# Hybrid decoder layer on one core: bias table written in the down-projection, other PSUM pairs for the third plain product, half-row token loads and a reordered first block of both feed-forward stages

## The chip, the cores and the metric

The program runs on one core of one Trainium2 chip, in one launch. The metric is the device time of the whole program in microseconds (us), the median of repeated executions. One further execution was recorded by the hardware profiler; all rows shown here are from that one.

## The reference, cut to what matters

One layer for 1024 prompt tokens and 8 sample tokens (1032 columns in all, width 1024, everything in float32): a feed-forward half step, a mixer (windowed attention and retention behind gates), a second feed-forward half step. A layer norm follows each of the three.

```
hp = layer_norm(ALPHA * hp + 0.5 * swiglu(hp, ffn1_w_up, ffn1_w_down), ln1_g, ln1_b)
mp = prompt_mixers(hp, w_in, sinks, rel_bias, w_attn_out, w_ret_out, w_o)     # likewise for the samples
hp = layer_norm(ALPHA * hp + mp, ln2_g, ln2_b)
hp = layer_norm(ALPHA * hp + 0.5 * swiglu(hp, ffn2_w_up, ffn2_w_down), ln3_g, ln3_b)

def swiglu(x, w_up, w_down):                 # w_up: 1024 x 5632, w_down: 2816 x 1024
    gate, up = split(x @ w_up, 2)
    return (silu(gate) * up) @ w_down
bias = rel_bias[rel_bucket(dist)]            # 8 heads, read by the windowed attention
```

## The kernel before, in words

**Operands.** Each float32 operand is split into a high part (`hi`, rounded to the matmul's format by ACT) and a low part (`lo = x - hi`, by DVE). A product is three matmuls: `w_hi*hi`, `w_hi*lo`, `w_lo*hi`. Weights arrive in halves of 128x512 (256 KB) in four buffers `raw`, are split into eight slots `w_hi`/`w_lo`, and are issued by SP's queue. A `raw` buffer is loaded again when the DVE split of its last use is through.

**The up-projections.** The 2816 hidden columns are 22 tiles (`ft` 0 to 21) of 128 gate and 128 up columns. The tokens are halved (`HT` = 516 columns) and so is the width: `ya` holds rows 0 to 511 of x, `yb` rows 512 to 1023, which gives four blocks b11, b12 (from `ya`) and b21, b22 (from `yb`). Tiles 1 to 21 use a seven-product scheme for 2x2 blocks: product units `P(ft, i)`, i = 0 to 6, each 24 matmuls of 128x258 with one of seven prepared token tiles `TT[i]` and one weight quarter or a sum of quarters (`st`, made by `sums` on DVE from the four `raw` buffers). Tile 0 is computed plainly as four units `C0` to `C3` of 48 matmuls, which need only tokens that are split and not summed; behind them DVE makes the sums that the other `TT` need. `t_stage(i)` emits the subtraction (in place in `ya`) and the two splits of one token tile.

The order of units, written by hand, is C0, C1, P(1,0), P(1,1), C2, C3, then P(1,3), P(1,2), P(1,4), P(1,5), P(1,6), P(2,0) and so on in order. C0 and C1 read TT[0] and TT[1], C2 and C3 TT[6] and TT[5].

**Accumulators.** Three PSUM pairs `pr[0..2]` take the products. C units alternate between pairs 0 and 2; P units of an odd tile use pair 1 for i = 0, 2, 4, 6, pair 0 for i = 1 and pair 2 for i = 3, 5 (an even tile swaps 0 and 1). A pair can be overwritten only when ACT or DVE has read it (the "evacuation").

**Order on the engines.** The program is emitted by hand in one pass. `Emit` keeps a modelled time `E.pe`, which decides only where a side task's instructions are placed; on the chip every engine takes its instructions in the order emitted. `before(ui, u)` emits what a unit needs ahead of it: token stages, weight splits (`need(o)`), and the functions held back until buffers are free (`held_th`: the gates; `held_ut`: stores).

**Side tasks.** `bias_tables` multiplies the head biases with a one-hot matrix and has POOL's queue write the result, widened, to a scratch tensor `scr` in DRAM: eight transfers of 128 rows of 1 KB. The attention reads it much later (`fill_att`). It starts when `E.pe` is over 60. `alpha_b` scales `yb` on POOL for the residual. `ln_last` is the layer norm of the last 264 columns ahead of the second feed-forward; `env["aside"]` is work that it lets in while it waits.

**The down-projections** take 4 hidden tiles a group in units of 12 matmuls into four PSUM banks `mb`, DVE adds each into `ya`/`yb`; weights come as before, 2 halves per 72 matmuls, and the activations are read back from DRAM (`T<-adr`).

```
order += [(1, i) for i in (3, 2, 4, 5, 6)]
order += [(ft, i) for ft in range(2, NF) for i in range(7)]
...
bank = pr[(al, 1 - al, al, 2, al, 2, al)[u["i"]] if u["kind"] == "P" else u["i"] % 2 * 2]
```

## Time and profile before

| | |
|---|---|
| median of 3 runs | 2252.5 us (2250.31 to 2253.45) |
| the profiled execution's own time | 2248.05 us |
| its span, first to last instruction | 2246.0 us |
| mean granted TensorE clock | 0.985 of full |
| PE busy | 2165.3 us (96% of the span) |
| DVE, ACT, POOL busy | 1369.7, 772.4, 236.0 us |
| PE's longest wait in the first 80 us, and the wait ahead of P(1,3) in the second feed-forward | 8.56 us, 4.51 us |

PE, the matmul engine, is the one that is nearly always at work, so what a change is worth is read from the places where PE stands still or runs at the lower clock. The count of matmuls in a stretch, held against the count in an undisturbed stretch, shows both at once. A row of the trace gives start, duration, engine, line, output and inputs, and in brackets how long the engine had been idle and what ended that.

### The profile page before, as it was taken

Reading aid. Unit: us, or ns where it says so; the run is one execution under the profiler, and the core shown is the slowest. Engines: PE = TensorE matmul, PEld = TensorE weight load, DVE = VectorE, ACT = ScalarE, POOL = GpSimd, SP = SyncE. Lnnn points to the kernel's source line nnn. Section 1 sums busy time; section 2 is a strip of 40 time slices with the busy share of each in tenths; the row PEclk is TensorE's granted clock in tenths of the full one; section 3 lists DMA queues with packets and bytes.
Section 4 is the critical chain, followed back from the end, with each engine's and each line's share of the span. In section 5 each row is a group of like instructions: output and inputs, shape, how many; then the busy total and the mean of one; then the engine's idle time right before and its main releaser. Section 6 shows DMA issues by size and latency. Waiting matters only on the chain.

```text
span 2246.0 us, 38320 instructions
## 1 busy us (share of the span) xinstructions
PE 2165.3 (96%) x15381; PEld 2133.5 (95%) x15381; DVE 1369.7 (61%) x2561; ACT 772.4 (34%) x1477; POOL 236.0 (11%) x290
## 2 busy tenths in 40 slices
PE   7979999999999899999999999997999999999996
PEld 6979999999999889999979999997999999999996
DVE  6746666654334887566665856778666666553337
ACT  4424333431111576111233443645434343411113
POOL 1200000001002434111110201111000000010003
PEclk8989999999999999999999999998999999999998
DMA  3553223357330210111164343541333233494212
GB/s 130 108 100 109 105 95 109 109 213 297 111 116 29 65 41 29 49 40 40 40 184 146 122 145 127 181 131 48 123 109 109 104 102 102 148 364 142 83 43 76
DMA packets 104851, 253.84 MB, mean 113 GB/s; under 512 B 13162, under 2 KB 16962, under 8 KB 98258
## 3 DMA queue, kind: packets, MB, share of 16 engines
q1 hardware_dynamic: 103970, 250.31, 32.5%
q0 software_dynamic: 704, 1.09, 1.5%
q8 instruction: 121, 1.98, 0.4%
q14 instruction: 56, 0.46, 0.1%
HBM read 194.95 MB, written 57.45 MB: 112 GB/s over the span
## 4 chain that ended last, share of the span: by engine, by line
PE 83%; DVE 8%; DMA 3%; ACT 3%; issue 2%; POOL 1%; SPq 0%; ACTq 0%; DVEq 0%; POOLq 0%
PE mb L90 43%; PE pr L90 37%; DMA raw<-in_w_dram 3%; PE sb L90 2%; DVE T L112 1%; DVE w_lo L112 1%; DVE ya L112 1%; DVE yb L112 1%; ACT w_hi L108 1%; DVE zt L112 1%; ACT T L108 1%; DVE ln L112 1%; PE mb L98 1%; DMA ya<-in_x_dram 0%; POOL pt L128 0%
## 5 line engine op out<-in xcount | busy, mean ns | idle before, releaser
L90 PE MATMUL mb<-T,w_hi 128*128 128x384 f32 (+1 forms) x3936 | 927.1, 323 | 1.8 <-DVE yb L112 1.8
L90 PE MATMUL pr<-T,w_hi 128*128 128x258 f32 x4960 | 814.6, 287 | 41.0 <-ACT a L108 14.7
L90 PEld LDWEIGHTS pr<-T,w_hi 128*128 128x128 f32 x4960 | 696.2, 193 | 45.1 <-ACT a L108 15.6
L90 PEld LDWEIGHTS mb<-T,w_hi 128*128 128x128 f32 x3936 | 677.3, 189 | 8.2 <-issue 3.7
L90 PE MATMUL mb<-T,w_lo 128*128 128x384 f32 (+1 forms) x1968 | 630.3, 320 | 0.0
L90 PE MATMUL pr<-T,w_lo 128*128 128x258 f32 x2480 | 506.3, 286 | 0.3 <-DVE w_lo L112 0.3
L108 ACT ACTIVATE w_hi<-raw 128x512 fp32r<-128x512 f32 x500 | 304.3, 624 | 481.4 <-PE mb L90 373.6
L112 DVE TENSOR_TENSOR w_lo<-raw,w_hi 128x512 fp32r<-128x512 f32 x500 | 354.2, 732 | 140.2 <-ACT w_hi L108 139.3
L90 PEld LDWEIGHTS pr<-T,w_lo 128*128 128x128 f32 x2480 | 392.0, 192 | 0.5 <-DVE w_lo L112 0.5
L90 PEld LDWEIGHTS mb<-T,w_lo 128*128 128x128 f32 x1968 | 370.5, 188 | 0.0
L112 DVE SCALAR_TENSOR_TENSOR ya<-mb,ya 128x384 f32<-128x384 f32 (+1 forms) x144 | 74.1, 515 | 134.5 <-PE mb L90 134.2
L112 DVE SCALAR_TENSOR_TENSOR yb<-mb,yb 128x384 f32<-128x384 f32 (+1 forms) x144 | 73.3, 514 | 124.3 <-PE mb L90 124.3
L112 DVE TENSOR_TENSOR a<-pr,a 128x516 f32<-128x516 f32 x87 | 60.5, 695 | 98.4 <-PE pr L90 94.7
L108 ACT ACTIVATE w_hi<-st 128x512 fp32r<-128x512 f32 x126 | 78.8, 628 | 91.6 <-PE pr L90 56.6
L132 POOL TENSOR_SCALAR ya<-ya 128x384 f32<-128x384 f32 (+1 forms) x24 | 12.2, 508 | 843.0 <-DMA ya<-hres 429.4
L112 DVE TENSOR_TENSOR w_lo<-st,w_hi 128x512 fp32r<-128x512 f32 x126 | 83.0, 686 | 0.0
L108 ACT ACTIVATE th<-a 128x516 f32<-128x516 f32 x43 | 27.3, 636 | 123.2 <-DVE a L112 123.2
L108 ACT ACTIVATE a<-pr 128x516 f32<-128x516 f32 x86 | 51.6, 600 | 39.6 <-PE pr L90 39.5
L90 PE MATMUL mb<-o_hi,w_hi 128*128 128x384 f32 (+1 forms) x192 | 61.9, 322 | 0.0
L90 PE MATMUL mb<-g_lo,w_hi 128*128 128x384 f32 (+1 forms) x192 | 61.4, 320 | 0.0
L90 PE MATMUL mb<-g_hi,w_lo 128*128 128x384 f32 (+1 forms) x192 | 61.2, 319 | 0.0
L90 PE MATMUL mb<-o_lo,w_hi 128*128 128x384 f32 (+1 forms) x192 | 61.2, 319 | 0.0
(317 smaller groups left out, 2041.0 us busy)
## 6 DMA issues: line engine op xcount, KB each, us to landing
raw<-in_w_dram SPq DMA_DIRECT2D x500, 256.0 KB, 2.9
T<-adr SPq DMA_DIRECT2D x44, 1032.0 KB, 9.5
adr<-ya SPq DMA_DIRECT2D x44, 516.0 KB, 2.9
adr<-ah SPq DMA_DIRECT2D x22, 516.0 KB, 2.6
adr<-m SPq DMA_DIRECT2D x22, 516.0 KB
out_yp_dram<-zt SPq DMA_DIRECT2D x16, 256.0 KB, 2.0
ya<-in_x_dram SPq DMA_DIRECT2D x2, 1032.0 KB, 7.4
yb<-in_x_dram SPq DMA_DIRECT2D x2, 1032.0 KB, 13.7
```

The costliest lines, as they stand in the source:

```text
L90: self.nc.tensor.matmul(out=out, lhsT=lhsT, rhs=rhs, start=start, stop=stop, **kw)
L98: self.nc.tensor.transpose(out=out, in_=in_, identity=ident)
L108: self.nc.scalar.activation(out=out, in_=in_, func=func, scale=scale, **kw)
L112: getattr(self.nc.vector, fn)(**kw)
L132: self.nc.gpsimd.tensor_scalar(out=out, in0=a, scalar1=s, scalar2=1.0, op0=ALU.mult, op1=ALU.mult)
```

## The change

Seven edits, in the order of the diff below.

1. In the order of units P(2,0) moves up, between P(1,4) and P(1,5).
2. In `ln_last` the matmul of the sums is placed 2.6 us of modelled time later among PE's products; the first 252 columns of the second half of `ya` are split (new `t_part`, stages 8 and 9) in the layer norm, where the weight sums stood; the weight sums (`aside`, without the two splits) come after the reciprocal root.
3. The tokens' first load is of half rows: four transfers of 128 x 2 x 516 for the first half of the tokens, then two of 128 x 4 x 516 for the second half.
4. In the second feed-forward the rest of b12 and b22 is split ahead of the held gates (`end_held` is a new function, called after `t_stage(9)` and `t_stage(5)`).
5. `bias_tables` starts at modelled time 560 instead of 60.
6. In the first feed-forward the token stages come later: stage 7 after the weights of C0, stage 2 at C2, stage 4 at C3; the weights of the next units come ahead of them. In the second one the weight splits of P(1,3) and P(1,2) come behind stage 4.
7. In the first feed-forward C2 writes pair 2 and C3 pair 0, the other way round from before.

```diff
-            order += [(1, i) for i in (3, 2, 4, 5, 6)]
-            order += [(ft, i) for ft in range(2, NF) for i in range(7)]
+            order += [(1, 3), (1, 2), (1, 4), (2, 0), (1, 5), (1, 6)]
+            order += [(ft, i) for ft in range(2, NF) for i in range(7) if ft > 2 or i]
...
-            yield t
+            yield max(t, E.pe + 2.6)
             b = yield from sbanks.get()
             E.mm(b[:, :N], onesm, env["lS"][0][:, :N], True, True)
...
-            env["aside"]()
+            t_stage(8)
             yield t
...
-            yield rsqrt(lv[:W, 0, :nb], lv[:W, 1, :nb], t)
+            t = rsqrt(lv[:W, 0, :nb], lv[:W, 1, :nb], t)
+            env["aside"]()
+            yield t
...
+        def first_x(k, i, n, a, b):
+            ds(out=env["yb" if k else "ya"][:, i:i + n, a:b], in_=xd[:, 4 * k + i:4 * k + i + n, a:b])
+
         for h in range(4):
             ds(out=raw[h], in_=half(I["w"][wrow[h // 2]].rearrange("p (k c) -> p k c", k=KD), h))
             arrive[h] = 0.0
             for i in (0, 2) if h < 2 else ():
-                ds(out=env["yb" if h else "ya"][:, i:i + 2], in_=xd[:, 4 * h + i:4 * h + i + 2])
+                first_x(h, i, 2, 0, HT)
+        for k in range(2):
+            first_x(k, 0, 4, HT, T)
...
+        def t_part(i, src, a, b):
+
+            hi, lo = (TT[i][:, o:o + 2 * T].rearrange("p (k n) -> p k n", k=4)[:, :, a:b] for o in (0, 2 * T))
+            t = E.act(hi, src[:, :, a:b], n=4 * (b - a))
+            tready[i] = E.tt(lo, src[:, :, a:b], f(hi), ALU.subtract, n=4 * (b - a), after=t)
...
+            early = CH[2][0] - HT
...
+            elif i == 7:
+                t_hl(6, b12)
+            elif i == 8:
+                t_part(6, b12, 0, early)
             else:
-                t_hl(6, b12)
+                t_part(6, b12, early, HT)
...
             *env["a"][2:], env["th"] = [env["ln"][:, i * HT:i * HT + HT] for i in range(4)]
+
+        def end_held():
             for fn in env.pop("held_th"):
                 fn()
...
-            yield 60.0
+            yield 560.0
             p = ctx_open("bt", R)
...
                     if i == 0:
-                        stages([] if p else [2], [0])
+                        need(o)
                     elif i == 1:
                         stages([], [1] if p else [1, 2, 3])
                     elif i == 3:
-                        stages([6] if not p else [4], [2] if p else [5, 6])
-                        if not p:
-                            end_t(p)
-                            env["busy"] = False
-                    elif i == 2 and p:
-                        stages([6], [4, 5])
-                    elif i == 4 and p:
+                        stages([4 if p else 6], [2, 3] if p else [6, 7])
+                    elif i == 2:
+                        stages([6] if p else [], [4, 5])
+                    elif i == 4:
                         end_t(p)
+                        if p:
+                            need(o + 6)
                         env["busy"] = False
...
-                        env["aside"] = lambda: (need(o + 6), need(o + 7))
+                        env["aside"] = lambda: sums(ops[o + 6]["quad"])
                     else:
                         need(o)
                         t_stage(0)
-                        t_stage(7)
                         need(o + 1)
                         t_stage(1)
                         need(o + 2)
                         need(o + 3)
+                        t_stage(7)
...
                 elif i == 2:
                     if p:
                         end_ln()
-                        t_stage(7)
+                        t_stage(9)
                         t_stage(5)
+                        end_held()
                     else:
-                        t_stage(4)
+                        t_stage(2)
...
                     else:
+                        t_stage(4)
                         need(o + 8)
...
-                bank = pr[(al, 1 - al, al, 2, al, 2, al)[u["i"]] if u["kind"] == "P" else u["i"] % 2 * 2]
+                bank = pr[(al, 1 - al, al, 2, al, 2, al)[u["i"]] if u["kind"] == "P" else (0, 2, 0, 2)[u["i"]] if u["p"] else (0, 2, 2, 0)[u["i"]]]
```

Three places show how instructions move. The first is DVE in the first feed-forward, from the evacuation of C1 to that of P(1,1). In these rows `a_126` is the activation of C0/C1, `a_127` that of P(1,0)/P(1,1), `pr_139` and `pr_141` are pairs 0 and 2, `T_108` and `T_117` are TT[2] and TT[4], `st` and `raw` are weight sums, `w_lo` weight splits.

```order
 L112 TENSOR_TENSOR a_126<-pr_141,a_126 128x516
-L112 TENSOR_TENSOR ya<-yb,ya 128x2x516 x2
-L112 TENSOR_TENSOR T_108<-ya,T_108 128x1032 x2
 L112 TENSOR_TENSOR st_123<-raw_83,raw_84 128x512
...
 L112 TENSOR_TENSOR a_127<-pr_139,a_127 128x516
 L112 TENSOR_TENSOR ya<-yb,ya 128x2x516 x2
+L112 TENSOR_TENSOR T_108<-ya,T_108 128x1032 x2
+L112 SCALAR_TENSOR_TENSOR a_127<-th,a_127 128x516
+L112 TENSOR_TENSOR ya<-yb,ya 128x2x516 x2
 L112 TENSOR_TENSOR T_117<-ya,T_117 128x1032 x2
-L112 SCALAR_TENSOR_TENSOR a_127<-th,a_127 128x516
```

Stage 2 (the subtraction into `ya` and the splits of T_108) moved from ahead of the weight sums and of the evacuation of P(1,1), `a_127<-pr_139`, to behind both. A little further on, the gate of C2 reads pair 2 (`pr_141`, before `pr_139`) and the evacuation of C3 pair 0.

The second place is POOL's queue from the start to the first layer norm; `oh` is the one-hot matrix, `rsb` the bias product, `yb` and `ya` the residual's scaling.

```order
-L920 DMA oh<-in_onehot_dram 32x256
-L928 DMA scr<-rsb 128x1x256
-L132 TENSOR_SCALAR yb<-yb 128x384 x2
-L132 TENSOR_SCALAR yb<-yb 128x264
...
-L928 DMA scr<-rsb 128x1x256 x7
-L132 TENSOR_SCALAR ya<-ya 128x384 x2
...
+L132 TENSOR_SCALAR ya<-ya 128x264
+L941 DMA oh<-in_onehot_dram 32x256
+L949 DMA scr<-rsb 128x1x256 x8
```

All eight writes of `scr` now stand behind both scalings, and nothing stands ahead of the scaling of `yb`; in between, nothing on POOL paces the eight.

The third place is DVE in the second feed-forward, between the evacuation of C3 (`ln<-pr_13620`, after the change `ln<-pr_13622`) and the weight split that P(1,4) waits for. `T_109` is TT[4], `T_13608` (after: `T_13610`) TT[6]. Before:

```order
L112 TENSOR_TENSOR ln<-pr_13620,ln 128x516
L112 TENSOR_TENSOR ya<-yb,ya 128x2x516 x2
L112 TENSOR_TENSOR T_109<-ya,T_109 128x1032 x2
L112 TENSOR_TENSOR ya<-yb,ya 128x2x516 x2
L112 TENSOR_TENSOR T_13608<-ya,T_13608 128x1032 x2
L112 TENSOR_TENSOR w_lo_74<-raw_83,w_hi_66 128x512
```

And of the change:

```order
L112 TENSOR_TENSOR ln<-pr_13622,ln 128x516
L112 TENSOR_TENSOR ya<-yb,ya 128x2x516 x2
L112 TENSOR_TENSOR T_109<-ya,T_109 128x1032 x2
L112 TENSOR_TENSOR w_lo_76<-st_13611,w_hi_68 128x512
L112 TENSOR_TENSOR w_lo_79<-st_13612,w_hi_71 128x512
L112 TENSOR_TENSOR ya<-yb,ya 128x2x516 x2
L112 TENSOR_TENSOR T_13610<-ya,T_13610 128x1032 x2
L112 TENSOR_TENSOR w_lo_74<-raw_83,w_hi_66 128x512
```

The weight splits of P(1,3) and P(1,2) (`w_lo_76`, `w_lo_79`), which stood in the layer norm before, now stand behind the splits of T_109.

## Rows read from the trace of the kernel before

**Rows 1.** The page, part 1: span, then busy time and share by engine.

```profile
span 2246.0 us, 38320 instructions
PE 2165.3 (96%) x15381; PEld 2133.5 (95%) x15381; DVE 1369.7 (61%) x2561; ACT 772.4 (34%) x1477; POOL 236.0 (11%) x290
```

**Rows 2.** Stretches: length, then busy (x instructions) by engine, PEclk, DMA share, GB/s.

```profile
0.00:80.00 80.00, 61.11 (x424) 57.83 (x425) 54.84 (x70) 36.19 (x52) 5.89 (x15) 0.89 0.35 118
120.00:130.00 10.00, 3.99 (x20) 3.77 (x19) 0.69 (x1) 1.12 (x2) 0.00 (x0) 0.70 0.92 42
120.00:150.00 30.00, 17.46 (x114) 17.04 (x113) 8.98 (x14) 6.25 (x12) 0.00 (x0) 0.77 0.60 103
210.00:220.00 10.00, 10.00 (x85) 10.00 (x85) 6.99 (x11) 4.49 (x7) 0.00 (x0) 1.00 0.34 132
617.00:653.00 36.00, 36.00 (x230) 36.00 (x229) 13.42 (x25) 3.79 (x6) 0.00 (x0) 1.00 0.29 100
```

**Rows 3.** Tile `raw`, 84 to 150 us: weight loads, from issue to landing.

```profile
L447 SPq DMA_DIRECT2D raw<-in_w_dram x11: 328/333/12809, 84.4 to 143.3; - x11
...
DMA to landing us min/median/max: 2.6/2.8/29.7
```

**Rows 4.** Tile `scr`, 80 to 200 us: the eight writes and their landing.

```profile
L928 POOL DMA_DIRECT2D scr<-rsb x8: 522/524/573, 91.2 to 104.2; - x8
...
DMA to landing us min/median/max: 6.3/17.4/30.9
```

**Rows 5.** PE in order of time: start, duration, instruction; the down-projection's first matmuls.

```profile
496.64 0.51 PE L90 MATMUL mb<-T,w_hi 128*128 128x384 f32 x2
```

**Rows 6.** SP's queue in order of time, 620 to 630 us: two weight loads.

```profile
623.07 2.55 SPq L447 DMA_DIRECT2D raw<-in_w_dram  x2
```

**Rows 7.** ACT in order of time, 640 to 660 us: splits of weights, one period apart.

```profile
643.07 0.63 ACT L108 ACTIVATE w_hi<-raw 128x512 fp32r<-128x512 f32 x1 [9.23 <-PE mb L90]
...
654.40 0.63 ACT L108 ACTIVATE w_hi<-raw 128x512 fp32r<-128x512 f32 x1 [9.23 <-PE mb L90]
```

**Rows 8.** ACT, 8 to 18 us: the split of the first half's last tokens.

```profile
17.06 1.06 ACT L108 ACTIVATE T<-yb 128x1032 fp32r<-128x1032 f32 x1 [1.11 <-DMA yb<-in_x_dram]
```

**Rows 9.** Stretches, columns as in rows 2: token loads; weight loads.

```profile
12.00:13.00 1.00, 1.00 (x6) 0.81 (x5) 0.93 (x2) 1.00 (x3) 0.00 (x0) 0.50 0.99 413
1430.00:1440.00 10.00, 10.00 (x84) 10.00 (x84) 6.58 (x14) 5.26 (x12) 0.00 (x0) 1.00 0.73 239
```

**Rows 10.** DVE in order of time, 24 to 42 us.

```profile
24.81 2.38 DVE L112 TENSOR_TENSOR T<-yb,T 128x1032 fp32r<-128x1032 f32 x2 [0.18 <-ACT T L108]
...
32.55 0.70 DVE L112 TENSOR_TENSOR a<-pr,a 128x516 f32<-128x516 f32 x1
33.17 2.37 DVE L112 TENSOR_TENSOR ya<-yb,ya 128x1032 f32<-128x1032 f32 x2
...
41.55 0.69 DVE L112 TENSOR_TENSOR a<-pr,a 128x516 f32<-128x516 f32 x1
```

**Rows 11.** PE in order of time: the starts of C2, P(1,3) and P(1,4).

```profile
42.30 1.01 PE L90 MATMUL pr<-T,w_hi 128*128 128x258 f32 x3 [8.56 <-DVE a L112]
...
56.47 0.72 PE L90 MATMUL pr<-T,w_hi 128*128 128x258 f32 x4 [0.88 <-DVE a L112]
...
64.30 0.76 PE L90 MATMUL pr<-T,w_hi 128*128 128x258 f32 x4 [1.82 <-ACT a L108]
```

**Rows 12.** PE, second feed-forward: the starts of C2, P(1,3) and P(1,4).

```profile
1526.24 0.80 PE L90 MATMUL pr<-T,w_hi 128*128 128x258 f32 x2 [0.47 <-DVE T L112]
...
1544.11 1.20 PE L90 MATMUL pr<-T,w_hi 128*128 128x258 f32 x4 [4.51 <-DVE ln L112]
...
1554.67 0.80 PE L90 MATMUL pr<-T,w_lo 128*128 128x258 f32 x2 [0.26 <-DVE w_lo L112]
```

**Rows 13.** DVE there: the evacuation of C3, and the last token tile's splits.

```profile
1543.27 0.70 DVE L112 TENSOR_TENSOR ln<-pr,ln 128x516 f32<-128x516 f32 x1
...
1550.95 2.85 DVE L112 TENSOR_TENSOR T<-ya,T 128x1032 fp32r<-128x1032 f32 x2
```

**Rows 14.** POOL: two scalings of the residual, one beside little else, one beside DVE.

```profile
516.75 6.87 POOL L132 TENSOR_SCALAR ya<-ya 128x384 f32<-128x384 f32 x12 [412.00 <-DMA ya<-in_x_dram]
...
1549.92 11.39 POOL L132 TENSOR_SCALAR yb<-yb 128x384 f32<-128x384 f32 x12 [36.98 <-DVE ya L112]
```

## The prediction, made before the changed kernel had run

> **What bounds the kernel now.** I read the page first: PE is busy in 96% of the span, DVE in 61% [rows 1], so the time is PE's, and a gain can only come from places where PE stands still or runs slow. The stretches find them by counting matmuls. Undisturbed, 10 us hold 85, one in 0.1176 us [rows 2]. The first 80 us hold 424 where 680 would fit: 256 missing, some 30 us. The 30 us from 120 hold 114 where 255 would fit: 141 missing, 16.6 us, with PE busy for 17.46 us and a granted clock of 0.77 [rows 2], so part of the loss is standing still and part the lower clock (1.2 of 2.4 GHz). The third place is the start of the second feed-forward, read from PE's rows in order of time: 4.51 us of wait ahead of P(1,3) [rows 12]. The three are what the change touches; I sum one term for each, against the profiled execution's own 2248.05 us, which is 4.45 us below the median of the runs, 2252.5. A difference under 0.2%, 4.5 us, can hardly be told from none here.
>
> **A: the bias table (edit 5).** What happens at 120: weight loads issued between 84 and 150 land after 2.8 us in the middle but up to 29.7 us, and one issue holds SP's queue for 12.8 us [rows 3]. In that time lie the eight writes of `scr`, issued at 91.2 to 104.2, landing after 6.3 to 30.9 us [rows 4], so until about 133. They are small (1 KB rows), and the DMA share is 0.60 at 103 GB/s over the 30 us, against 0.34 at 132 GB/s undisturbed [rows 2]. One unit of this stage reads four halves and has nothing to do without them. With the writes away, I count the whole 16.6 us as gained.
>
> Where they go: the order puts 756 matmuls of the down-projection ahead of the bias matmul. That stage starts at 496.64 [rows 5] and 72 of its matmuls take 11.33 us, the distance of two like splits [rows 7]: 756 x 11.33/72 = 119, so the writes start at about 616 in the time of before. All eight are now issued back to back, so the clash lasts about as long as it took from the first seven-fold issue to the last landing, some 30 to 36 us: 617 to 653. There PE has no idle time, at full clock, and the DMA share is 0.29 [rows 2]. Loads issued there at 623.07 [rows 6] are split from 643.07 on [rows 7]: 20 us of cover. If a load takes the 29.7 us of before, 9.7 us are uncovered; DVE's additions from the banks queue behind the late weight split, and the four banks of 12 matmuls (4 x 12 x 11.33/72 = 7.6 us) cushion some of it. So the cost lies between 0 (it lands in 20 us) and 9.7 us, and a few more if the clock falls as at 120. I take 3, a third of the way, because this stage moves 100 GB/s where the other moved 132 undisturbed [rows 2], so less stands beside the writes. The next users of `scr` come much later, in the attention. A = -16.6 + 3 = **-13.6** (-16.5 to -7).
>
> **B: the first 80 us (edits 1, 3, 6, 7).** The last piece of the first half's tokens is split at 17.06, on landing [rows 8]. Ahead of its landing stand 4640 KB now (all tokens, 4128, and two weight halves), and 2576 KB after. At the 413 GB/s of token loads [rows 9] the 2064 KB less make 5.1 us: 12.0. Rows of 2064 bytes may be slower; weight loads have rows of 2048, and moved 239 GB/s at a share of 0.73, 327 at a full one [rows 9], which makes it 13.4. The second half then lands last, at 18.3 to 21 (the same two rates), and its split on DVE, at 24.81 before [rows 10], begins at 21.5 to 24.
>
> From there DVE is the chain. Ahead of C1's evacuation stand now: this split 2.4, a subtraction 2.4, a split 2.4, a gate 0.7, the evacuation 0.7 (durations of rows 10); the end is 30.0 to 32.6, against 33.25 before. What waits for it is larger: C2 wrote pair 0, which P(1,1) fills, and stood 8.56 us until 42.30 [rows 11] for that evacuation at 41.55 [rows 10]. After the change it writes pair 2, which C1 leaves, and may start at 30 to 33. Then the token sums for P(1,3) bound. DVE has: weight sums and two splits 3.7, evacuation 0.7, subtraction and split of T_108 4.7, gate 0.7, subtraction and split of T_117 4.7, a weight split 0.6, a gate 0.7, in sum 15.8 to 16. P(1,3) starts at 46.0 to 48.7, before 56.47 [rows 11]. The moved units then take 6.7 (P(1,3), P(1,2)), 0.6 (an evacuation by ACT), 11.3 (four units of 24 at 0.1176), and a new wait: with P(2,0) moved up, (1,6) and (2,1) stand next to each other on pair 1, and (2,1) waits for an evacuation of about 1.8. So (2,1) starts at 66.4 to 69.1. Before it came four units behind P(1,4): 64.30 [rows 11] + 11.3 = 75.6. B = -6.5 to -9.2; I take **-7.5**, nearer the slow token rate because the rows are as short as the weights', and put the bounds at -4 and -10.
>
> A rule of the Trainium skill speaks against this. POOL's scaling of `yb` (12 instructions) stood behind the first bias write, at 91.79; nothing holds it now, and it falls at about 52 to 63, into DVE's chain. Beside a busy DVE it took 11.39 us, alone 6.87 [rows 14], and DVE's pair of splits beside it 2.85 instead of 2.38 [rows 13, 10]. Five or six such DVE operations lie in that window: about +1 us, mostly under PE's products. The page "SBUF — State Buffer", section "SBUF: two separate sides", says that the two engines share a port pair as an exclusive lock, and that a DVE operation with two SBUF inputs and a GpSimd one that reads SBUF block each other fully. By that DVE would lose POOL's own 6.9 us there. The row shows a fifth, not a full block; this is a rival below.
>
> **C: the second feed-forward's start (edits 2, 4, 6).** With the sums behind the reciprocal root, the layer norm's last step comes some 2 us sooner, and part of C2's tokens are split ahead; C2 starts at about 1522.4 instead of 1526.24 [rows 12]. DVE would reach the evacuation of C3 by 1538 instead of 1543.27 [rows 13], but two weight splits that stood in the layer norm now follow the splits of T_109, and P(1,3) waits for the first of them: 1538.3 + 0.7 + 4.7 makes about 1543.7, where it started at 1544.11 [rows 12]. P(1,4) waits for a weight split behind one more token tile: about 1551.8 instead of 1554.67 [rows 12]; its own units go on from there. Off that comes 0.9 for (1,6) and (2,1) side by side. I take C = **-2.5**, between +1 (all of the lead is lost to the moved splits) and -6 (P(1,3) starts by all of the 4 us sooner).
>
> Sum: -13.6 - 7.5 - 2.5 = -23.6, 2224.4 for an execution like the profiled one, and **2229** on the median's scale.
>
> **Rivals.** R1, the clash goes along: PE waits in the down-projection for weights 9.7 us and loses some 3 more to the clock. Speaks for: the cover is 20 us and the worst landing 29.7. Against: half of the loads. 9.7 more than my 3: 2239. 18%.
> R2, POOL's scaling blocks DVE wholly in the first feed-forward. For it: the page; against it: rows 13 and 14 as read above. 6.9 us less from B, a little of it hidden: about 2235. 6%.
> R3, C gives nothing or costs 1: 2231.5 to 2232.5; within the range of my forecast.
> R4, all bounds on the good side (no stall in A, -10 in B, -6 in C): -32.6, 2220. 9%.
> R5, the other side: the half-row token loads run at the rate of small pieces. The stretch of the bias writes, of 1 KB rows, moved 42 GB/s at a share of 0.92 [rows 2]; twice the row would make 84, so 4128 KB take 50 us, the last tokens land near 55, P(1,3) starts near 80 instead of 56.5, 24 us late instead of 7.5 early, and the sum is -13.6 + 24 - 2.5 = +7.9: 2260. It decides from about 27 us of lateness of the second half on. Against it: 2 KB rows of weights at 327 GB/s [rows 9]. 3%.
>
> My forecast has 64%, with its own range 2222 to 2235. The 8-in-10 range takes in R4, R2 and most of R1: 2216 to 2240. Only R5 is not faster; with 2% for an unnamed wash, faster 0.95, same 0.02, slower 0.03.
>
> **What would show it.** In the trace after: no gap of PE near 120, and 85 matmuls per 10 us there; `scr` written about 590 to 625 (the earlier stages being 24 us shorter), and in that stage loads landing 20 to 30 us late, with PE's or `mb`'s waits behind them, if R1 holds. ACT's split of the last first-half tokens at 12 to 13.5; C2 at 30 to 33, P(1,3) at 46 to 49, (2,1) at 66 to 69 with a wait of 1 to 2 us. DVE's durations beside POOL's scaling near 52 to 63: 2.85 for a pair by my reading, far more by R2. In the second feed-forward P(1,3) waiting for a weight split, not for an evacuation. I am wrong if PE's wait at P(1,3) in the first block stays near 56, if a gap shows in the down-projection, or if the second half of the tokens lands past 27.

## The result and the profile after

The changed kernel takes 2232.57 us (median of 4 runs, 2228.13 to 2236.5), the kernel before 2252.4 (4 runs): a ratio of 0.9913, 95% interval 0.9893 to 0.9932. The forecast was 2229, range 2216 to 2240. The profiled execution took 2232.96 us, 15.1 less than that of before, where 23.6 less were summed. The page, part 1, as in [rows 1]:

```profile
span 2231.0 us, 38311 instructions
PE 2158.0 (97%) x15381; PEld 2125.4 (95%) x15381; DVE 1370.6 (61%) x2561; ACT 772.1 (35%) x1477; POOL 238.0 (11%) x290
```

The stretches, columns as in [rows 2]; the last one is new, where the down-projection meets the bias writes:

```profile
0.00:80.00 80.00, 67.15 (x494) 64.10 (x495) 64.25 (x82) 40.59 (x59) 15.97 (x26) 0.96 0.40 136
120.00:150.00 30.00, 30.00 (x250) 30.00 (x249) 18.75 (x28) 12.08 (x20) 0.00 (x0) 1.00 0.28 99
620.00:640.00 20.00, 11.01 (x60) 10.86 (x59) 3.43 (x6) 1.37 (x3) 0.00 (x0) 0.74 0.68 143
```

The first 80 us hold 70 matmuls more than before. The gap at 120 to 150 is gone: 250 matmuls at full clock instead of 114. But 20 us of the down-projection, which had none missing before, are busy for 11.01 us at a clock of 0.74.

**Where the time went.** Five marks that every trace has cut the program into stretches: PE's first matmul of the first down-projection, of the first layer norm's sums, of the second feed-forward, of the second down-projection, and the end of the span. Lengths in us, the first from the start of the span:

| kernel | to the down-projection | to the layer norm | to feed-forward 2 | to its down-projection | to the end |
|---|---|---|---|---|---|
| before | 496.64 | 223.35 | 776.56 | 473.70 | 275.75 |
| after | 470.81 | 234.66 | 777.43 | 472.14 | 275.96 |
| difference | -25.83 | +11.31 | +0.87 | -1.56 | +0.21 |

Terms A and B without the new clash came out 1.7 us better than summed (-24.1), the clash cost 11.3 instead of 3, and C gave 1.6 in this pair of traces instead of 2.5. The middle stretch (777 us here) has the same work in all kernels and was 776.3 to 780.6 long over the 13 traces of this study; that alone can set two traces some 4 us apart, so the kernels below are read by stretches first.

**The first block.** PE in order of time: C2, P(1,3), (2,1), and the first matmul of the down-projection, against [rows 11] and [rows 5]:

```profile
30.26 0.74 PE L90 MATMUL pr<-T,w_hi 128*128 128x258 f32 x4 [2.68 <-DVE a L112]
...
45.80 0.99 PE L90 MATMUL pr<-T,w_hi 128*128 128x258 f32 x3 [3.67 <-DVE a L112]
...
67.39 0.73 PE L90 MATMUL pr<-T,w_hi 128*128 128x258 f32 x4 [1.60 <-DVE m L112]
...
470.81 0.51 PE L90 MATMUL mb<-T,w_hi 128*128 128x384 f32 x2
```

ACT's split of the last first-half tokens, then DVE's split of the second half and C1's evacuation, against [rows 8] and [rows 10]:

```profile
12.02 1.07 ACT L108 ACTIVATE T<-yb 128x1032 fp32r<-128x1032 f32 x1 [0.30 <-DMA yb<-in_x_dram]
...
21.76 2.38 DVE L112 TENSOR_TENSOR T<-yb,T 128x1032 fp32r<-128x1032 f32 x2 [0.26 <-ACT T L108]
...
29.51 0.70 DVE L112 TENSOR_TENSOR a<-pr,a 128x516 f32<-128x516 f32 x1
```

All of these lie in the forecast's bands, or 0.2 us ahead of them. In before, (2,1) starts at 76.01:

```profile
76.01 0.64 PE L90 MATMUL pr<-T,w_hi 128*128 128x258 f32 x4
```

So by 67.39 the kernel is 8.6 us ahead. P(1,3), after its wait of 3.67, runs at half clock until 49.0; that matters where runs are compared there.

**The down-projection.** The eight writes (tile `scr`, 500 to 760 us), as in [rows 4]:

```profile
L949 POOL DMA_DIRECT2D scr<-rsb x8: 522/522/550, 592.3 to 596.0; - x8
...
DMA to landing us min/median/max: 7.3/21.7/34.2
```

The last has landed at 596.0 + 34.2 = 630.2. PE, ACT and DVE around that time:

```profile
608.10 0.63 ACT L108 ACTIVATE w_hi<-raw 128x512 fp32r<-128x512 f32 x1 [0.83 <-PE mb L90]
...
623.55 0.34 PE L90 MATMUL mb<-T,w_hi 128*128 128x384 f32 x1
630.95 0.63 ACT L108 ACTIVATE w_hi<-raw 128x512 fp32r<-128x512 f32 x1 [22.22 <-DMA raw<-in_w_dram]
631.62 0.69 DVE L112 TENSOR_TENSOR w_lo<-raw,w_hi 128x512 fp32r<-128x512 f32 x1 [11.64 <-ACT w_hi L108]
632.22 0.55 DVE L112 SCALAR_TENSOR_TENSOR yb<-mb,yb 128x384 f32<-128x384 f32 x1
632.88 0.48 PE L90 MATMUL mb<-T,w_hi 128*128 128x384 f32 x1 [8.99 <-issue]
```

The weights are late: splits come in pairs every 11.33 us, one pair was due at 606.63 + 11.33 = 617.96, and it came at 630.95. But that is not what PE stood for. Its last matmul before the wait, at 623.55, is the first of a unit of 12, the third unit that uses the weights split at 606.6 and 608.1 (the first starts at 619.35, and 24 matmuls take 4.2 us), and the releaser of the next is "issue": nothing that the profile shows. What was missing is seen in the DMA queues, packets, MB and share, first from 600 to 630, then from 630 to 636 us:

```profile
q0 software_dynamic: 318, 0.84, 83.2%
q1 hardware_dynamic: 308, 0.57, 5.7%
...
q1 hardware_dynamic: 499, 0.92, 46.2%
q8 instruction: 2, 0.03, 2.0%
```

And the instruction queue alone, from 581 to 630 us:

```profile
q8 instruction: 1, 0.02, 0.1%
```

Queue q8 fetches instructions, 121 packets and 1.98 MB in the whole program, 16 KB each. Taken microsecond by microsecond it shows one packet in each of those from 521, 542, 560, 581, then none until 630 and 634: where a block used to come every 20 us, none came for 49. That they are PE's blocks is read from their pace: 121 for 15381 matmuls make 127 a block, and 127 take 20.0 us here (72 in 11.33) and 14.9 in the up-projection (0.1176 each), where the blocks of 122 to 200 us come every 15.5. POOL's writes (q0) held 83% of the DMA engines meanwhile. The Trainium skill, page "Runtime: NRT & Kernel Launch", section "Instruction fetch mechanics", says that an engine's instruction memory is refilled in 16 KiB blocks by a DMA queue of its own and that the cost of a block boundary is mostly hidden. The block size agrees with these rows (1.98 MB in 121 packets); hidden it is in the rest of this trace, where PE has no other wait of over 0.5 us with the releaser "issue", but not here.

After the wait of 8.99 PE ran at half clock until 636.0 (the first matmul pairs there take 0.84 us instead of 0.51), which costs 1.6 more: the 72 matmuls from 619.35 last until 641.27, 21.92 us instead of 11.33. The last 0.7 of the 11.3 is there in e3 too (below), where PE has no such wait: 224.08, and 223.35 in before.

**The second feed-forward.** PE at C2, P(1,3) and P(1,4), with ACT ahead of P(1,3), against [rows 12], and last PE at (2,1) and inside it. As in [rows 12], the rows of C2 and P(1,4) are not the units' first ones but lie about 1.1 us behind their starts:

```profile
1507.24 0.51 PE L90 MATMUL pr<-T,w_hi 128*128 128x258 f32 x2 [0.60 <-DVE T L112]
...
1524.26 2.21 ACT L108 ACTIVATE T<-ya 128x1032 fp32r<-128x1032 f32 x2 [3.84 <-DVE ya L112]
1526.37 1.14 ACT L108 ACTIVATE w_hi<-st 128x512 fp32r<-128x512 f32 x2
1527.04 1.23 PE L90 MATMUL pr<-T,w_hi 128*128 128x258 f32 x4 [8.25 <-ACT w_hi L108]
...
1537.21 0.80 PE L90 MATMUL pr<-T,w_lo 128*128 128x258 f32 x2 [0.40 <-DVE w_lo L112]
...
1550.92 0.72 PE L90 MATMUL pr<-T,w_hi 128*128 128x258 f32 x4 [0.88 <-DVE ya L112]
...
1555.89 0.39 PE L90 MATMUL pr<-T,w_lo 128*128 128x258 f32 x1 [0.99 <-DVE w_lo L112]
```

Counted from PE's first matmul of the stage (1482.90 here, 1496.55 before), C2 is 5.4 us ahead of before, P(1,3) 3.4, P(1,4) 3.8 and (2,1) 2.6, and 1.6 are left at the down-projection. So P(1,3) gives back 2 of C2's lead: 8.25 us of wait instead of 4.51, for a weight split that stands on ACT behind the split of a token tile that P(1,3) does not read. The rest goes at (2,1), to the wait of 0.88 that edit 1 brings and to one of 0.99 for a weight split.

### The profile page after: what moved, and what is told of

It reads as the page before. It is cut to its first block, busy times and chain, and to the rows that moved or that the text cites. A ratio compares the mean times of both kernels' runs of the same rounds, so it can differ in the third digit from the quotient of the medians.

```text
span 2231.0 us, 38311 instructions
## 1 busy us (share of the span) xinstructions
PE 2158.0 (97%) x15381; PEld 2125.4 (95%) x15381; DVE 1370.6 (61%) x2561; ACT 772.1 (35%) x1477; POOL 238.0 (11%) x290
## 3 DMA queue, kind: packets, MB, share of 16 engines
q8 instruction: 121, 1.98, 0.4%
## 4 chain that ended last, share of the span: by engine, by line
PE 84%; DVE 8%; issue 2%; ACT 2%; DMA 2%; POOL 1%; SPq 0%; DVEq 0%; POOLq 0%; ACTq 0%
PE mb L90 44%; PE pr L90 38%; PE sb L90 2%; DMA raw<-in_w_dram 2%; DVE w_lo L112 1%; DVE T L112 1%; DVE ya L112 1%; DVE yb L112 1%; DVE zt L112 1%; DVE ln L112 1%; ACT T L108 1%; PE mb L98 0%; ACT w_hi L108 0%; PE sb L98 0%; POOL pt L128 0%
## 5 line engine op out<-in xcount | busy, mean ns | idle before, releaser
L90 PE MATMUL pr<-T,w_hi 128*128 128x258 f32 x4960 | 806.4, 285 | 23.3 <-ACT w_hi L108 8.3
L90 PEld LDWEIGHTS pr<-T,w_hi 128*128 128x128 f32 x4960 | 688.9, 191 | 26.4 <-ACT w_hi L108 8.8
L112 DVE TENSOR_TENSOR ln<-pr,ln 128x516 f32<-128x516 f32 x43 | 29.9, 695 | 58.1 <-PE pr L90 58.0
## 6 DMA issues: line engine op xcount, KB each, us to landing
T<-adr SPq DMA_DIRECT2D x44, 1032.0 KB, 11.2
```

The costliest lines, as they stand in the source:

```text
L90: self.nc.tensor.matmul(out=out, lhsT=lhsT, rhs=rhs, start=start, stop=stop, **kw)
L112: getattr(self.nc.vector, fn)(**kw)
```

## The experiments

Lengths are those of the table above; "to the down-projection" is 470.81 in after.

**e1: the bias table moved, nothing else** (on the kernel before).

```diff
-            yield 60.0
+            yield 560.0
```

> The kernel before with one edit: the bias table starts at modelled time 560 instead of 60. Theory (the trace after read by segments): PE's waits at 120 to 141 go, 17.6 us, and about 11.3 us come back as a wait of PE for weights in the down-projection, at about 645 us, so 2246 us, 6 less than before; the start of P(1,3) stays at 56.5. Rival 1, the forecast's term A: only 3 us come back, 2239. Rival 2: the waits at 120 come from the weight loads themselves and stay, 2252.

Measured: 2240.05 us, ratio 0.995 (0.9938 to 0.9963). To the down-projection 480.34, 16.3 less, and PE has 415 matmuls in 100 to 150 us where before had 279: the gap at 120 was the bias writes. The stretch to the layer norm is 226.87, only 3.5 longer. So alone the edit did what term A said (-16.3 + 3.5 = -12.8; -13.6 forecast), and theory 1's 11.3 is no constant: the same writes cost 3.5 here and 11.3 in after. PE's one wait there is short:

```profile
635.28 0.44 PE L90 MATMUL mb<-T,w_lo 128*128 128x384 f32 x1 [1.68 <-issue]
```

Here the last instruction block ahead of the writes came at 590 and the next at 633: 43 us without one, not 49 as in after. Of the rest of the 3.5 us, 0.58 is a wait for DVE's addition into `yb`, which stood behind the late split (638.09), and 0.7 is there in e3 too.

**e2: the bias table back to its old place** (on after).

```diff
-            yield 560.0
+            yield 60.0
```

> The kernel after with the bias table back at modelled time 60. Theory: the gains of the two starts stay (8.2 and 1.1 us), the waits at 100 to 145 come back, the one in the down-projection goes: 2239 to 2243 us. POOL's scaling of the residual then stands behind a bias write, outside DVE's chain of the first block, so this shows too what POOL cost there: (2,1) starts at 66.4 to 67.4 if the slow-down of DVE beside POOL is as small as 2.85 for 2.38, at about 60 to 61 if POOL held DVE up for its whole time.

Measured: 2236.99 us, ratio 0.9939 (0.9926 to 0.9951). The wait of the down-projection is gone (223.36 to the layer norm, 223.35 before), and one of 9.99 us is back:

```profile
127.85 1.23 PE L90 MATMUL pr<-T,w_hi 128*128 128x258 f32 x4 [9.99 <-ACT a L108]
```

The time is 2 us under the theory's 2239 to 2243. To the down-projection it is 484.18, 13.4 more than after. So moving the table, within the whole change, gained 13.4 - 11.3 = 2.1 us by stretches. (2,1) starts at 67.62, with POOL's scaling out of the way (at 86.17), and at 67.39 in after with the scaling beside it: POOL cost the path nothing. One reason is its place: in after it starts at 47.75, when P(1,3) has begun, so it lies behind the part of DVE's chain that sets P(1,3). What it did to DVE shows in one pair, first in after, with POOL's row, then in e2:

```profile
47.75 11.11 POOL L132 TENSOR_SCALAR yb<-yb 128x384 f32<-128x384 f32 x12 [39.00 <-DVE ya L112]
48.79 2.85 DVE L112 TENSOR_TENSOR T<-ya,T 128x1032 fp32r<-128x1032 f32 x2
```

```profile
48.93 2.38 DVE L112 TENSOR_TENSOR T<-ya,T 128x1032 fp32r<-128x1032 f32 x2
```

**e3: the eight writes paced** (on after). ACT makes a source for each write, between its weight splits.

```diff
+            rsc = [p.tile([8, 256], F32, name=f"rsc{i}") for i in range(4)]
...
-                dq(out=dst[h:h + 1], in_=rsb[h:h + 1].unsqueeze(1).to_broadcast([1, P, 256]))
-                yield E.pe + 8.0
+                E.act(rsc[h % 4], rsb, n=256)
+                dq(out=dst[h:h + 1], in_=rsc[h % 4][h:h + 1].unsqueeze(1).to_broadcast([1, P, 256]))
+                yield E.pe + 11.3
```

> The kernel after; each of the eight bias writes gets a source of its own (a copy of the bias by ACT, four buffers) that ACT makes one by one between weight splits some 11 us apart, so that the writes no longer queue up. Theory, the burst is what delays the loads: each write lands within 7 us or so, loads land inside their 20 us of cover, no wait of PE in the down-projection, 11 us less than after: 2221 to 2222 us. Rival, each write alone holds the transfers up long enough: PE still waits, in several smaller pieces, 2226 to 2233.

Measured: 2225.85 us, ratio 0.9887 (0.9873 to 0.99). Tile `scr`:

```profile
L951 POOL DMA_DIRECT2D scr<-rsc x8: 524/524/550, 593.1 to 666.2; - x8
...
DMA to landing us min/median/max: 6.3/6.3/7.3
```

No wait of PE of over 0.4 us, 224.08 to the layer norm: 10.6 of the 11.3 us are back, and between 600 and 630 two instruction blocks arrive. The burst was what cost, not the eight writes as such. The median lies above the theory's 2221 to 2222, but of the waits that the rival expects none is there.

**e4: the same writes from 128 partitions** (on after).

```diff
-            E.mm(b[:8, :256], rb, oh, True, True)
+            E.mm(b[:, k * 256:k * 256 + 256], rb[:, h + k:h + k + 1].to_broadcast([32, P]), oh, True, True)
...
-                dq(out=dst[h:h + 1], in_=rsb[h:h + 1].unsqueeze(1).to_broadcast([1, P, 256]))
+                dq(out=dst, in_=bc[:, h])
```

> The kernel after; the bias is computed on all 128 partitions (each head's column of the table broadcast in the matmul), so that a write of scr takes its 128 rows of 1 KB from 128 partitions instead of 128 times from one; sizes, rows in DRAM, queue and time of issue as before. Theory 1, reading one partition 128 times makes the writes slow: the eight land within 10 us, no wait of PE in the down-projection, 2221 to 2222 us. Theory 2, 1 KB rows written to DRAM are slow from anywhere: landing up to 30 us and the wait of 9 us stay, 2232.

Measured: 2227.86 us, ratio 0.9901 (0.9887 to 0.9914). Theory 1 holds:

```profile
L953 POOL DMA_DIRECT2D scr<-bc x8: 539/539/587, 593.4 to 597.2; - x8
...
DMA to landing us min/median/max: 2.8/3.8/4.2
```

The same 1 MB in the same rows of DRAM, issued as fast, lands in 4.2 us at most instead of 34.2. The queue's packets took 31.5% of 16 engines for 100 us in after and 26.3% for 13 us here. In both traces they are 256 of 4 KB, which hold the data, and 128 of 4 bytes; one of 4 KB took 2.0 us in the mean in after and 0.21 here (after moved its 1.05 MB in 36 us, 29 GB/s). Neither the size of the rows nor DRAM made the writes slow, but reading one partition 128 times. It is not the best version: the stretch to the layer norm is 228.76, 5.4 more than in before. The broadcast matmuls hold PE from 591.4 to 595.0, and PE runs at half clock until 599.1.

**e5: the pairs back** (on after): C2 on pair 0, C3 on pair 2.

```diff
-                bank = pr[(al, 1 - al, al, 2, al, 2, al)[u["i"]] if u["kind"] == "P" else (0, 2, 0, 2)[u["i"]] if u["p"] else (0, 2, 2, 0)[u["i"]]]
+                bank = pr[(al, 1 - al, al, 2, al, 2, al)[u["i"]] if u["kind"] == "P" else (0, 2, 0, 2)[u["i"]]]
```

> The kernel after with C2 and C3 of the first feed-forward back on pairs 0 and 2 (edit 7 undone, all else kept). By the trace after, P(1,1)'s evacuation ends at 34.5, so C2 starts at 34.6 instead of 30.3. Theory, DVE's chain sets P(1,3): C2 and C3 take 11.9, the evacuation 0.7, P(1,3) starts at 47.2 instead of 45.8, so 1.4 us lost. Rival, the banks are what held C2 and all behind it: 4.3 us lost at P(1,3) and (2,1).

Measured: 2235.08 us, ratio 0.993 (0.9916 to 0.9943). C2 starts at 34.58, (2,1) at 68.96, 1.6 later, and the down-projection 1.6 later. That is the theory's size, but not its way there:

```profile
48.77 0.73 PE L90 MATMUL pr<-T,w_hi 128*128 128x258 f32 x4 [0.88 <-DVE a L112]
```

P(1,3) starts 3.0 later than in after (theory 1.4, rival 4.3), as C2 ran at half clock until 37.9 after its wait of 6.99. Then P(1,3) and P(1,2) run at full clock and P(1,4) follows 6.8 us behind P(1,3), where it took 8.1 in after: 1.4 come back from the clock. This trace also settles what PE stood for in the down-projection. PE, ACT and DVE:

```profile
625.13 0.34 PE L90 MATMUL mb<-T,w_hi 128*128 128x384 f32 x1
631.31 0.48 PE L90 MATMUL mb<-T,w_hi 128*128 128x384 f32 x1 [5.84 <-issue]
...
632.22 1.26 ACT L108 ACTIVATE w_hi<-raw 128x512 fp32r<-128x512 f32 x2 [21.91 <-DMA raw<-in_w_dram]
...
632.88 0.69 DVE L112 TENSOR_TENSOR w_lo<-raw,w_hi 128x512 fp32r<-128x512 f32 x1 [11.32 <-ACT w_hi L108]
```

PE goes on at 631.31, before the late weights are split at all, and just after an instruction block arrives (in the microsecond from 629, the first since the one from 582). It did not wait for weights.

**e6: whole-row token loads again** (on after).

```diff
-                first_x(h, i, 2, 0, HT)
-        for k in range(2):
-            first_x(k, 0, 4, HT, T)
+                first_x(h, i, 2, 0, T)
```

> The kernel after with whole-row token loads (edit 3 undone). Theory of the forecast: the last piece of the first half lands 5 us later (split at 17 instead of 12.0), C0 ends about 4 us later, and DVE's split of the second half's tokens, 21.76 after, begins at 24.8 as before; all behind it is 3 us later, (2,1) at 70.4, 3 us lost. Rival: the chain begins with the second half's tokens, which land last in either case, so at most 1 us is lost.

Measured: 2237.26 us, ratio 0.9938 (0.9924 to 0.9953). (2,1) at 68.94, the down-projection at 472.38: 1.6 us lost, between theory (3) and rival (at most 1).

**e7: P(2,0) back behind P(1,6)** (on after).

```diff
-            order += [(1, 3), (1, 2), (1, 4), (2, 0), (1, 5), (1, 6)]
+            order += [(1, 3), (1, 2), (1, 4), (1, 5), (1, 6), (2, 0)]
```

> The kernel after with P(2,0) back behind P(1,6) (edit 1 undone). Theory: the moved unit only put (1,6) and (2,1) side by side on one pair; without it the waits of 1.60 (first feed-forward) and 0.88 (second) ahead of (2,1) go, 1 to 2.5 us gained. Rival: P(2,0) filled time in which P(1,5) or P(1,6) would wait for a token tile or a weight split; then a wait of 1 to 3 us stands ahead of one of them in each feed-forward, 0 to 4 us lost.

Measured: 2230.11 us, ratio 0.9911 (0.9898 to 0.9925), by time alone no different from after. By stretches the down-projection starts at 467.77, 3.0 us sooner, and neither wait ahead of (2,1) is left:

```profile
52.72 0.75 PE L90 MATMUL pr<-T,w_hi 128*128 128x258 f32 x4 [0.69 <-ACT a L108]
...
64.42 0.64 PE L90 MATMUL pr<-T,w_hi 128*128 128x258 f32 x4
```

These are P(1,4), at 53.94 in after, and (2,1), at 67.39. Not all of the 3.0 us is edit 1's: 1.2 of it stands at P(1,4), ahead of the moved unit, because P(1,3) ran at full clock here and at half clock in after. The other 1.8 come between P(1,4) and (2,1), 1.6 of them the wait. So edit 1 lost 1.8 us in the first feed-forward; in the second the stretch is 471.75 (472.14 in after), within its scatter.

**e8: weight splits ahead of the token stage** in the second feed-forward (on after).

```diff
-                        stages([4 if p else 6], [2, 3] if p else [6, 7])
+                        if p:
+                            stages([], [2, 3])
+                        stages([4 if p else 6], [] if p else [6, 7])
```

> The kernel after; in the second feed-forward the weight splits of P(1,3) and P(1,2) stand ahead of the last but one token stage again (as the kernel before had them, early), not behind it. Theory: P(1,3), which stands 8.25 us for a weight split on ACT that is behind the split of a token tile it does not need, starts about 3 to 4 us sooner; P(1,4) waits for DVE's later tiles and gains 1 to 2.5, as DVE's idle 2.35 us ahead of its last split pair go: 1 to 2.5 us gained in the whole. Rival: P(1,4)'s chain on DVE is the same length plus two weight splits ahead, so nothing is gained.

Measured: 2232.42 us, ratio 0.9921 (0.9908 to 0.9933); the stretch is 472.92. The rival: PE's wait at P(1,3) falls from 8.25 to 4.46 us, and the next one, at P(1,4), grows from 1.23 to 3.31. As the rival has it, DVE's chain to the later token tiles binds; no run shortens that chain, so this is read and not tried.

**e9: the writes paced and P(2,0) back** (e3 and e7 together, on after; their two edits).

> The version that the runs so far point to: the kernel after with the eight bias writes paced by ACT (as in e3) and P(2,0) back behind P(1,6) (as in e7). If the two are independent: 2225.9 less the 3.0 us that the down-projection began earlier in e7, 2222 to 2223 us, about 27 to 29 less than before. Rival: they overlap, no better than 2225.9.

Measured: 2218.66 us, ratio 0.9863 (0.9848 to 0.9878), the fastest of all: 30.7 us under before in the same session, where after was 19.8 under it in its own. To the down-projection 469.25, to the layer norm 224.06. Against e3 that is 1.8 us sooner, all of it between P(1,4) (54.19; 54.24 in e3) and (2,1): edit 1's own price again, and less than the 3.0 that were expected. The two kernels' intervals touch (0.9873 and 0.9878), so by time alone e9's lead over e3 isn't clear.

**e10: the pairs alone** (on e1; the reverse of e5's edit).

> The kernel before with the bias table at 560 (as in e1) and edit 7 alone: C2 on pair 2, C3 on pair 0. Theory, the pair is what held C2 in the old order: C2 starts at about 33 instead of 41.6, DVE's idle 6.8 us between 47 and 56 go, P(1,3) starts near 50 instead of 57, the down-projection begins 5 to 7 us sooner than in e1 (480.3). Rival, by the 1.6 us that undoing it cost in e5: DVE's sums set P(1,3) anyway, 1 to 2 us.

Measured: 2235.76 us, ratio 0.9933 (0.992 to 0.9946). To the down-projection 475.88, 4.5 less than e1; PE runs on into C2 at 33.97 with no wait, P(1,3) starts at 50.20, 6.8 sooner than in e1 (56.98):

```profile
50.20 0.72 PE L90 MATMUL pr<-T,w_hi 128*128 128x258 f32 x4 [0.33 <-DVE a L112]
...
59.30 0.75 PE L90 MATMUL pr<-T,w_hi 128*128 128x258 f32 x4 [3.09 <-ACT a L108]
```

Nearer to the theory (5 to 7): of the 6.8 us, 0.8 goes to a longer wait at P(1,4) (3.09 instead of 2.24), and 1.5 to half clock behind it, from 60.4 to 63.9.

**e11: the stages of the first feed-forward back** (on after; the whole of edit 6 there).

```diff
-                        need(o)
+                        stages([] if p else [2], [0])
...
                         t_stage(0)
+                        t_stage(7)
                         need(o + 1)
                         t_stage(1)
                         need(o + 2)
                         need(o + 3)
-                        t_stage(7)
...
```

> The kernel after with edit 6 undone in the first feed-forward only (token stages 7, 2 and 4 and the weight splits where the kernel before has them); banks, loads, order and bias as after. Theory: DVE has the same operations ahead of P(1,3) in another order, so with the banks changed P(1,3) still starts at 45.8 to 47 and at most 1.5 us are lost. Rival: the early token stages push P(1,1)'s evacuation and C3's weights back; P(1,3) starts near 50, 4 us lost or more.

Measured: 2238.94 us, ratio 0.9956 (0.9942 to 0.997). The theory fell. The rival has the direction and the "or more", but not the place: the down-projection starts at 480.47, 9.7 us later, as late as in e1, which has none of the edits 1, 3, 6 and 7, and the loss begins ahead of C0. ACT and PE show why:

```profile
8.79 1.16 ACT L108 ACTIVATE T<-ya 128x516 fp32r<-128x516 f32 x2 [2.24 <-DMA ya<-in_x_dram]
16.28 2.02 ACT L108 ACTIVATE T<-ya 128x1032 fp32r<-128x1032 f32 x2 [6.33 <-DMA ya<-in_x_dram]
...
19.82 0.80 PE L90 MATMUL pr<-T,w_hi 128*128 128x258 f32 x2 [7.92 <-ACT T L108]
```

With half-row loads the second half's tokens come last, and the old order has ACT split them (stage 7) ahead of `yb`'s first half, which C0 reads. ACT stands 6.33 us for them and PE 7.92. Edits 1, 3 and 7 without edit 6 are worth nothing together, though edit 7 alone gained 4.5 in e10.

## Why the prediction was right, and where it was off

**Term A, the gap at 120** (-16.6): right; e1 shows -16.3 for the move alone.

**Term A, the clash** (0 to 9.7, taken 3): this step failed in its size. In e1 it came to 3.5, in after to 11.3, beyond the 9.7 and within the "few more" that the text left open for the clock. By the prediction's own sign, a gap in the down-projection, the step was wrong. The sum asked only when weight loads land. They came 13 us late where 9.7 was the worst that it saw, and DVE's additions queued behind them as said. Left out was another thing that comes by DMA, PE's instructions. R1's place was right and its price near (9.7 and 3 for the clock, 12.7 against 11.3 measured); "waits for weights" was not, by e5, so the price was near by luck. What would have been lost to the weights alone is an estimate: four banks let PE run until about 628 (619.5 and four units of 12 x 0.174 us), and the first bank came free behind the late split at 632.8, so some 5 us. In e11, where PE never lacked a block and the weights came 10 us late, the whole price against e3 is 2.1 (226.14 and 224.08), 1.81 of it a wait for DVE's addition into `yb`.

**Why 3.5 and 11.3.** The longest time without an instruction block between 555 and 660 us, to the microsecond, beside PE's wait in the down-projection whose releaser is "issue":

| | e3, e4 | e11 | e1 | e5, e10 | after, e6, e8 | e7 |
|---|---|---|---|---|---|---|
| us without a block | at most 23 | 28 | 43 | 47 | 49 | 50 |
| wait, us | none | none | 1.68 | 5.84, 5.79 | 8.99, 8.98, 8.72 | 8.71 |

The stop belongs to a place in the program and not to a time: in after, e5, e6, e7 and e8 PE stands after the same matmul, the 961st of the down-projection, in e1 and e10 after the 962nd. In all seven it stops 42 to 43 us after the start of the last block's packet and goes on 2.2 to 2.5 us after the start of the next one's. So the wait is what the time without a block has over 40 to 41 us, and the price hangs on when the next block gets through: in good time in e11 (619.6), 4 and 2 us ahead of the end of the burst in e1 and e5, at its end or up to 0.6 us behind it in the other five. What lets a block through is open. Where in the 20 us between two blocks the burst begins does not decide it: it began 9.3 us after a block in e1 and in e10, with waits of 1.68 and 5.79, and 11.2 and 11.3 in e5 and after, with 5.84 and 8.99. All this is read from these ten traces; no run moved the burst alone.

**Term B** (-7.5, bounds -4 and -10): -8.6 at (2,1), as before's (2,1) stands at 76.01 and not at the 75.6 that was added up, and -9.5 at the down-projection against e1, which has edit 5 alone. Its steps lie on their rows: the split at 12.02 (12.0 to 13.4), DVE's at 21.76, C2 at 30.26, P(1,3) at 45.80, the new wait 1.60 (1.8). The reason given for C2, the pair, holds in the old order (e10: 4.5 us); in the new one it is worth 1.6 (e5; 3.0 at P(1,3), of which the clock gives back 1.4), as DVE's sums bind behind it, which the text said too. What the text did not see is that the parts hang together: 1.6 for the pairs, 1.6 for the loads, 9.7 for the stages when each is undone alone, and 1.8 lost by edit 1, whose effect it did name, the wait ahead of (2,1).

**Term C** (-2.5, +1 to -6): -1.6 in the pair of traces; over the seven traces with after's code there and its order of units, e8 apart, the stretch is 472.55 in the mean, over the three with before's code (before, e1, e10) 473.52, so -1.0. The seven run from 471.6 to 474.3 and the three from 472.6 to 474.3, so no gain is shown, and by the means R3 (nothing) was nearer than the forecast. P(1,3) does wait for a weight split, but on ACT; it and P(1,4) started sooner than worked out (3.4 and 3.8 ahead instead of 0.4 and 2.9). The sum missed what comes behind them: beside the 0.9 at (2,1) that it took off, a wait of 0.99 for a weight split inside (2,1).

**R2**, POOL holding DVE: refuted by e2, and the scaling fell at 47.75, not at 52, behind what sets P(1,3). The Trainium skill, page "SBUF — State Buffer", section "SBUF: two separate sides", would have the two block each other fully, and by its words for one instruction at a time. The rows don't contradict that: POOL's 12 operations, 0.57 us each alone, took 11.11 us (6.87 alone [rows 14]), and DVE's beside them up to 0.3 us more each (the pair 2.85 instead of 2.38, weight splits 0.89 to 0.99 instead of 0.69). What the rival had wrong is the price, POOL's whole 6.9 us on top of DVE's chain; DVE's operations became 1.9 us longer in all. **R5**, slow half rows: refuted, the first half was there at 12.0 and the second's split at 16.07 on ACT.

So the total was right by errors that partly cancel: A and B 1.7 us better than summed, the clash 8.3 worse, C 0.9 worse, the two stretches that no term covered 1.1 worse, and the median's step from the profiled execution (4.45 in before, -0.4 in after) took some of it back.

## What to carry to other kernels

A slow burst of transfers that is moved under another stage still has a price: list everything there that comes by DMA, with its cover, the instruction blocks of the busiest engine among them. Spread the burst out (e3) or make it fast at its source (e4) rather than only move it. Edits to loads and to the order that consumes them belong together, and each part of a change that pays is worth undoing alone: here one of them cost 1.8 us (e7, e9). Before a difference of a few us is put down to an edit, the granted clock of the stretch has to be compared: it made 1.2 of e7's 3.0 us.

## What the runs showed of the hardware that was not expected

PE can run out of instructions: no 16 KB block for 49 us while a DMA queue of slow packets held 83% of the engines, where one came every 20 us, and PE stood 9.0 us in after and 5.8 in e5, where its operands were there. A DMA that reads one partition 128 times moved packets of 4 KB at 2.0 us each, 29 GB/s in all, the same rows from 128 partitions at 0.21. The middle stretch came out 776.3 to 780.6 us long with the same work, in two groups (to 777.4 in seven traces, from 778.5 in the other six); why stays open.
